# Token mixings: the first value weights lie where head outputs come later, and are queued ahead of the residual's stores and the stacking copies

## The chip, the core and the metric

The kernel runs on one core of a Trainium2 chip. The metric is the time of one execution in device microseconds (us), as the median of several runs. The engines are PE (matmul), DVE (vector), ACT (activation), POOL and SP; SP computes nothing here and issues the DMAs, one after the other.

## What is computed

The reference runs two residual blocks on 512 tokens of width 1024 and then two layers of a second network. Each of these layers is a feed-forward block, a token mixing and a second feed-forward block. The change touches the token mixing, which runs twice (mixing 0 and mixing 1):

```python
def token_mixing(h, w_in, rel_bias, lq1, lk1, lq2, lk2, subln_g, w_out, lambda_init):
    proj = h @ w_in
    qa, ka, va, qb, kb, vb, qc, kc, vc = jnp.split(proj, ...)
    o_a = chunk_band_attention(qa, ka, va, rel_bias)                       # 6 heads of 64
    o_b = diff_attention(qb, kb, vb, lam, subln_g, lambda_init)            # 4 heads of 64
    o_c = stick_breaking_attention(qc, kc, vc)                             # 6 heads of 64
    y = jnp.concatenate([o_a, o_b, o_c], axis=-1)
    return y @ w_out
```

The result is normed and added to the residual x, and the second feed-forward block follows.

## The kernel before

Activations lie with the features on the partitions: x is 8 tiles of 128 x 512 tokens. Every operand of a matmul is split into a high and a low part (xH and xL, wh and wl), and each product is three matmuls (`mm3`, L141 to L146: high by high, low by high, high by low).

**Weights.** All weights of the program stand in one list in the order of their use. `wload` (L74) loads the list up to a given entry, and `wnext` (L124) takes the next entry and loads four ahead. An entry is two tiles of 128 x 1024 (512 KB each), wh and wl, from a ring of five pairs; a load waits until the matmuls of the entry five before it have read their tiles. The weights of the mixings were split into halves earlier and stored in DRAM, so an entry of a mixing is two plain DMAs (L87), both issued by SP. In this text w0 to w3 are the first four entries of a mixing (the query and key weights of the head pairs 0 and 1), w4 to w7 the value weights of the first eight heads, and w8 the query weight of head pair 2.

**The start of a mixing** (`mix`, L1103). While the tail of the feed-forward block before it still updates x on DVE, PE does the projections with w0 to w3 (`head4`, L325, tile names p), in two halves of the tokens. SP stores the new x to DRAM (L1113, eight DMAs of 256 KB, spill), since the value tile V takes the memory of x. Each projection is then scaled on DVE (qkf, L1138), split by ACT and DVE (hl, L233 and L234) and copied, high and low parts stacked on 128 partitions, to the tiles sq and sk by SP's DMAs (`stack`, L1132): 24 copies of 128 KB for the first four projections. Only two hl tiles are there, so the third split waits for the copies of the first.

**The value projection** (`vproj`, L1161, tile names pv) uses w4 to w7 twice, for each half of the tokens: 2 x 48 matmuls of 512 columns into two PSUM banks, which ACT and DVE empty into V (L1177, L1178) after each half.

**The heads.** Each head has score matmuls (pS, L1186, 8 of them), maxima on DVE (L1209), exponentials on ACT (L1225), 10 transposes on PE (pT, L1245), a split of the transposed probabilities on ACT and DVE (pH, pL) and the output matmuls (pO, L1256). The projections of later heads (pq) are interleaved with the steps of the heads. The outputs of a head pair, split again, go to a tile O of 128 x 2 x 512. The first six, O0 to O5, are allocated at the start of the mixing:

```python
        O = {i: o_p.tile([P, 2, T], F32R, name=f"O{i}") for i in range(6)}
```

The order on each engine is set by a scheduler from the program and its dependencies, not by the order of the source alone.

Of the kernel before, what the change touches and what calls it, by code (L numbers as in the profile page):

```python
# [10 lines left out]
F32R = mybir.dt.float32r  # L11
# [6 lines left out]
P = 128  # L18
T = 512
# [8 lines left out]
def f(ap):  # L28
    return ap.bitcast(F32)


class Net:
# [6 lines left out]
    def __init__(s, ctx, tc, I, cols, dram):  # L39
        s.ctx, s.tc, s.nc, s.I, s.cols, s.dram = ctx, tc, tc.nc, I, cols, dram  # L40
        s.spill = dram.tile([P, 8, T], F32, name="spill")
        pool = lambda name, bufs=1, **k: ctx.enter_context(tc.tile_pool(name=name, bufs=bufs, **k))
        s.cp = pool("const")
        s.wp = pool("w", 5)
        s.xp = pool("x")
        s.ap = pool("acc")
        s.tp = pool("tiny", 2)
        s.pp = pool("ps", 1, space=PSUM)
        s.psum(mm=range(6), t=(6, 7))
        s.held, s.free = "x", "fb"  # L50
        s.wq, s.wi, s.ready, s.loaded, s.jobs, s.due, s.rate = [], 0, {}, 0, [], 0, 2.2
        s.early = []
        nc = s.nc
        s.w_eng = nc.vector
        s.ident = s.cp.tile([P, P], F32, name="ident")
        s.ones = s.cp.tile([P, P], F32, name="ones")
        nc.vector.memset(s.ones, 1.0)
        s.vecs = s.cp.tile([P, I["vecs"].shape[1]], F32, name="vecs")
        nc.sync.dma_start(s.vecs, I["vecs"])
# [14 lines left out]
    def wload(s, upto):  # L74
        nc = s.nc
        while s.loaded < min(upto, len(s.wq)):
            ap, n, hl = s.wq[s.loaded]
            if not hl:
                st = s.wp.tile([P, 1024], F32, tag="ws", name="ws", bufs=2)
                nc.sync.dma_start(st[:, :n], ap)  # L80
            wh = s.wp.tile([P, 1024], F32R, tag="wh", name="wh")
            wl = s.wp.tile([P, 1024], F32R, tag="wl", name="wl")
            s.ready[s.loaded] = (wh, wl)
            s.loaded += 1
            if hl:
                for x, w in enumerate((wh, wl)):
                    nc.sync.dma_start(f(w[:, :n]), hl[:, x])  # L87
                continue
            nc.scalar.activation(wh[:, :n], st[:, :n], AF.Copy)  # L89
            s.w_eng.tensor_tensor(wl[:, :n], st[:, :n], f(wh[:, :n]), op=ALU.subtract)  # L90
            s.due = s.due + s.rate if s.jobs else 0
            while s.jobs and s.due >= 1:
                s.jobs.pop(0)()
                s.due -= 1
# [706 lines left out]
    def cd(s, X, C):  # L801
# [122 lines left out]

        s.psum(S=range(3), T=(3, 4, 5), O=(6,), mm=(7,))
        ap = pool("cda")
# [70 lines left out]
        def pv(hf):  # L997
            h, half = hf // 2, hf % 2
            b = h % 2
            if half == 0:  # L1000
                pOs[h] = s.bank("pO", "O")
            pO = pOs[h]
# [100 lines left out]
    def mix(s, l, st, mktail):  # L1103
# [3 lines left out]
        op = ExitStack()  # L1107
        s.psum(mm=(0, 1), S=(2, 3, 4, 7), O=(5,), t=(6,))
        s.w_eng = nc.gpsimd
        o_p = op.enter_context(tc.tile_pool(name="mo", bufs=1, reuse_waits="tile"))  # L1110
        a_p = op.enter_context(tc.tile_pool(name="ma", bufs=1, reuse_waits="tile"))
        for k in range(8):
            nc.sync.dma_start(s.spill[:, k], s.x[:, k])  # L1113

# [5 lines left out]
        nlam = s.tp.tile([P, 1], F32, tag="nlam", name="nlam")  # L1120
        nc.vector.scalar_tensor_tensor(nlam, ll[:, 1:2], -lam0, ll[:, 0:1], op0=ALU.add, op1=ALU.subtract)

        O = {i: o_p.tile([P, 2, T], F32R, name=f"O{i}") for i in range(6)}
        V = {}
        qk = {}

        def hl():

            return a_p.tile([P, 2, T], F32R, tag="hl", name="hl", bufs=2)
# [99 lines left out]
        def pv_head(z, hd):  # L1229
            side = not 6 <= hd < 10  # L1230

            v = V[hd // 8][0]
            pO = s.bank("pO", "O")
            vt = lambda j: v[:, j, hd % 8].rearrange("p a d -> p (a d)")
# [26 lines left out]
        def o_add(pO, hd):  # L1261
            e, pr = hd % 2, hd // 2
            if e == 0:
                OT[pr] = a_p.tile([P, T], F32, tag="OT", name="OT", bufs=1)
            a, b = slice(64 * e, 64 * e + 64), slice(64 - 64 * e, 128 - 64 * e)
            o = OT[pr][a]
            nc.scalar.activation(o, pO[b], AF.Copy)
            nc.vector.tensor_tensor(o, pO[a], o, op=ALU.add)
            if e == 0:
                return  # L1270
            if pr < 5:
                bc = s.bcast2(rcs.pop(pr).rearrange("p i b -> p (i b)"), "t")
                nc.vector.tensor_tensor(OT[pr], OT[pr], bc, op=ALU.mult)
            if 3 <= pr < 5:
                sub_norm(pr)
            if pr >= 6:
                O[pr] = hl()
            s.split(O[pr][:, 0], O[pr][:, 1], OT[pr])

        def head_a(h):  # L1280
            tab = a_p.tile([P, T], F32, tag="tab", name="tab", bufs=2)
            nc.sync.dma_start(tab, s.I["rel"][l, h])
            z, nm = maxes(("a", h // 2), h % 2, 0, tab)
            yield
            rc(h)
            exps(z, nm, rcs[h // 2][:, :, h % 2])
            yield
            o_add(pv_head(z, h), h)

        def head_b(h):  # L1290
            tab = a_p.tile([P, T], F32, tag="tab", name="tab", bufs=2)
            nc.sync.dma_start(tab, s.I["alibi"][h])
            key = ("b", h // 2)
            m0 = maxes(key, h % 2, 0, tab)
            m1 = maxes(key, h % 2, 1, tab)
            yield
            z0, z1 = m0[0], m1[0]
            hd = 6 + h
            rc(hd)

            q = s.tp.tile([P, 4], F32, tag="rq", name="rq")
            s0 = exps(*m0, rcs[hd // 2][:, :, h % 2])
            exps(*m1, q)
            nc.vector.scalar_tensor_tensor(q, q, nlam, s0, op0=ALU.mult, op1=ALU.mult)
            for i in range(4):
                nc.vector.scalar_tensor_tensor(zs(z0, i), zs(z1, i), q[:, i:i + 1], zs(z0, i), op0=ALU.mult, op1=ALU.add)
            yield
            o_add(pv_head(z0, hd), hd)

        def sub_norm(pr):  # L1310
            ot = OT[pr]
            sq = s.ap.tile([P, T], F32, tag="md", name="osq")
            nc.scalar.activation(sq, ot, AF.Square)
            ps = s.bank("sn", "t")
            for t in range(4):
                nc.tensor.matmul(ps[:, 2 * t:2 * t + 2], sq[:, t * P:(t + 1) * P], s.hsel, start=True, stop=True)
            v = s.tp.tile([P, 8], F32, tag="snv", name="snv")
            nc.vector.tensor_scalar(v, ps[:, 0:8], 1.0 / 64, 1e-6, op0=ALU.mult, op1=ALU.add)
            y = s.rsqrt(v, 8, "sn")
            ps = s.bcast2(y, "t")  # L1320
            g = s.hg[f"subln_{l}"]
            nc.vector.scalar_tensor_tensor(ot, ot, g, ps, op0=ALU.mult, op1=ALU.mult)

        def head_c(h):
            key = ("c", h // 2)
            nb, be = ztile(), ztile()
            for i in range(4):
                n = (i + 1) * P
                ps = scores(key, h % 2, 0, i, stop=False)
                nc.tensor.matmul(ps[:, i * P:n], s.identr, s.maskr, start=False, stop=True)  # L1330
                nc.scalar.activation(zs(nb, i), ps[:, :n], AF.Sigmoid, scale=-1.0)
                nc.scalar.activation(zs(be, i), ps[:, :n], AF.Sigmoid)
                nc.gpsimd.memset(zs(nb, i, 1)[:, n:], 1.0)
            yield
            for i in range(4):
                nbi = zs(nb, i)
                nc.vector.tensor_tensor_scan(nbi[:, ::-1], nbi[:, ::-1], nbi[:, ::-1], 1.0, op0=ALU.mult, op1=ALU.bypass)
                nc.vector.tensor_tensor(zs(be, i), zs(be, i), zs(nb, i, 1)[:, 1:], op=ALU.mult)
            yield
            hd = 10 + h  # L1340
            o_add(pv_head(be, hd), hd)
# [288 lines left out]
```

## Time and profile before

| what | value |
|---|---|
| median of 3 runs | 2776.08 us (2770.22 to 2778.55) |
| profiled execution, its own time | 2773.9 us |
| its span in the profile | 2772.1 us |
| mean granted TensorE clock | 0.978 |
| PE busy | 2637.8 us, 95% |
| DVE, ACT, POOL busy | 1506.4, 1057.8, 322.3 us |
| chain that ended last | PE 76%, DVE 13%, ACT 3%, DMA 3% |

The span is the time from the first to the last instruction of the profiled execution; the difference of 1.8 us to its own time lies around it. The clock is a share of 2.4 GHz. A wait is the idle time of an engine just before an instruction, with what ended it in angle form ("<- DMA wh<-hl" is a load of a wh tile from hl in DRAM). "ws<-", "wh<-", "wl<-" name a DMA by the tile that it writes and what it reads.

### The profile page before, as it was taken

What the parts mean: (1) busy time and instruction counts of PE and PEld (TensorE: products, weight loads), DVE (VectorE), ACT (ScalarE), POOL (GpSimd) and SP (SyncE); (2) the same over time, 40 slices, a digit from 0 to 9 for tenths busy, and PEclk for the clock granted to TensorE, in tenths of its full rate; (3) what the DMA queues carried; (4) which work ended last, traced back from release to release, by engine and by line L of the source; (5) the groups of instructions that cost most, each with busy time, mean ns of one, the idle gap of its engine ahead of it and who ended that gap; (6) DMA issues with size and microseconds to landing.
All of it is one profiled execution on the core that took longest, in us unless ns stands there. A gap on an engine that the chain in (4) does not pass through costs nothing.

```text
span 2772.1 us, 36203 instructions
## 1 busy us (share of the span) xinstructions
PE 2637.8 (95%) x13676; PEld 2229.2 (80%) x13676; DVE 1506.4 (54%) x2886; ACT 1057.8 (38%) x1951; POOL 322.3 (12%) x300
## 2 busy tenths in 40 slices
PE   7898999998999998999999999999998998999998
PEld 6787987887888886877888888888886877888887
DVE  7885632888545353675853436634335467642334
ACT  4122543765443232444542224433223355432222
POOL 2324343002000020001200002000001000300000
PEclk9999999999999998999999999999999999999999
DMA  7353123005897246654693223962235665232321
GB/s 268 133 183 127 44 86 98 28 32 188 296 324 270 93 143 194 194 159 153 205 309 122 94 89 103 322 216 99 96 110 183 205 197 152 70 106 92 99 91 62
DMA packets 133966, 418.15 MB, mean 151 GB/s; under 512 B 17376, under 2 KB 20960, under 8 KB 133792
## 3 DMA queue, kind: packets, MB, share of 16 engines
q1 hardware_dynamic: 133792, 415.84, 45.3%
q8 instruction: 108, 1.77, 0.3%
q14 instruction: 66, 0.54, 0.1%
HBM read 314.32 MB, written 73.40 MB: 140 GB/s over the span
## 4 chain that ended last, share of the span: by engine, by line
PE 76%; DVE 13%; ACT 3%; issue 3%; DMA 3%; SPq 1%; POOL 0%; DVEq 0%; ACTq 0%; POOLq 0%
PE pd L146 6%; PE pd L145 6%; PE pd L144 6%; PE pg L144 5%; PE pg L145 5%; PE pg L146 5%; PE pu L145 5%; PE pu L146 5%; PE pu L144 5%; DVE junk L472 2%; PE pO L1256 1%; PE pq L144 1%; DVE x L310 1%; PE pq L145 1%; PE pq L146 1%
## 5 line engine op out<-in xcount | busy, mean ns | idle before, releaser
L89 ACT ACTIVATE wh<-ws 128x1024 fp32r<-128x1024 f32 (+2 forms) x335 | 345.6, 1034 | 865.5 <-PE pd L145 242.1
L90 DVE TENSOR_TENSOR wl<-ws,wh 128x1024 fp32r<-128x1024 f32 (+1 forms) x267 | 318.1, 1192 | 165.0 <-ACT wh L89 161.6
L144 PE MATMUL pg<-xH,wh 128*128 128x512 f32 x672 | 262.3, 390 | 0.0
L146 PE MATMUL pg<-xH,wl 128*128 128x512 f32 x672 | 261.7, 389 | 0.0
L145 PE MATMUL pg<-xL,wh 128*128 128x512 f32 x672 | 261.7, 389 | 0.0
L146 PE MATMUL pd<-hH,wl 128*128 128x512 f32 x632 | 249.7, 395 | 0.0
L144 PE MATMUL pd<-hH,wh 128*128 128x512 f32 x632 | 249.6, 395 | 0.0
L145 PE MATMUL pd<-hL,wh 128*128 128x512 f32 x632 | 249.6, 395 | 0.0
L145 PE MATMUL pu<-xL,wh 128*128 128x512 f32 x640 | 249.2, 389 | 0.0
L144 PE MATMUL pu<-xH,wh 128*128 128x512 f32 x640 | 249.1, 389 | 0.0
L146 PE MATMUL pu<-xH,wl 128*128 128x512 f32 x640 | 249.0, 389 | 0.0
L90 POOL TENSOR_TENSOR wl<-ws,wh 128x1024 fp32r<-128x1024 f32 (+1 forms) x68 | 171.1, 2522 | 328.7 <-ACT wh L89 320.9
L244 POOL TENSOR_TENSOR accf<-accf,sq 128x256 f32<-128x256 f32 x48 | 39.6, 846 | 1388.3 <-ACT sq L243 1388.3
L396 DVE TENSOR_TENSOR ht<-ht,pu 128x512 f32<-128x512 f32 x80 | 54.8, 685 | 183.4 <-PE pu L146 181.3
L146 PEld LDWEIGHTS pg<-xH,wl 128*128 128x128 f32 x672 | 126.1, 188 | 26.2
L144 PEld LDWEIGHTS pg<-xH,wh 128*128 128x128 f32 x672 | 126.2, 188 | 26.1
L145 PEld LDWEIGHTS pg<-xL,wh 128*128 128x128 f32 x672 | 126.2, 188 | 25.9
L146 PEld LDWEIGHTS pd<-hH,wl 128*128 128x128 f32 x632 | 118.6, 188 | 28.8
L145 PEld LDWEIGHTS pd<-hL,wh 128*128 128x128 f32 x632 | 118.6, 188 | 28.8
L144 PEld LDWEIGHTS pd<-hH,wh 128*128 128x128 f32 x632 | 118.6, 188 | 28.6
L144 PEld LDWEIGHTS pu<-xH,wh 128*128 128x128 f32 x640 | 120.1, 188 | 25.1
L146 PEld LDWEIGHTS pu<-xH,wl 128*128 128x128 f32 x640 | 120.1, 188 | 24.9
(616 smaller groups left out, 5978.5 us busy)
## 6 DMA issues: line engine op xcount, KB each, us to landing
ws<-ffn_gate SPq DMA_DIRECT2D x88, 512.0 KB, 3.5
ws<-ffn_up SPq DMA_DIRECT2D x88, 512.0 KB, 3.5
hl<-eh SPq DMA_DIRECT2D x64, 512.0 KB, 7.2
hl<-el SPq DMA_DIRECT2D x64, 512.0 KB, 6.8
ws<-ffn_down SPq DMA_DIRECT2D x64, 512.0 KB, 3.7
wh<-hl SPq DMA_DIRECT2D x64, 512.0 KB, 4.5
wl<-hl SPq DMA_DIRECT2D x64, 512.0 KB, 5.9
es<-wqk SPq DMA_DIRECT2D x32, 512.0 KB, 6.0
```

Of the source, the lines that this page charges most:

```text
L89: nc.scalar.activation(wh[:, :n], st[:, :n], AF.Copy)
L90: s.w_eng.tensor_tensor(wl[:, :n], st[:, :n], f(wh[:, :n]), op=ALU.subtract)
L144: mm(out, A[0], B[0], start=start, stop=False)
L145: mm(out, A[0], B[1], start=False, stop=False)
L146: mm(out, A[1], B[0], start=False, stop=stop)
L244: (eng or nc.gpsimd).tensor_tensor(acc[0], acc[0], sq, op=ALU.add)
L310: nc.vector.scalar_tensor_tensor(s.x[:, k, sl], fk, s.hg[post][:, k:k + 1], s.x[:, k, sl], op0=ALU.mult, op1=ALU.add)
L396: nc.vector.tensor_tensor(t, t, pu, op=ALU.mult)
L472: nc.vector.tensor_tensor_reduce(j, w, fbt[:, v * 1024:(v + 1) * 1024], 1.0, 0.0, op0=ALU.mult, op1=ALU.add, accum_out=dst[:, m, v:v + 1])
L1256: nc.tensor.matmul(o, vt(j), p[:, j, c0:], start=(x == 0 and j == 0), stop=(x == 1 and j == nj - 1))
```

## The change

At the start of a mixing the entries w4, w5 and w6 get homes of their own: the six tiles O0 to O5, two for each entry, under the name wV. The load of everything up to w7 is asked for there, ahead of the stores of x. The tiles of the outputs are allocated when a head pair is done, with the same tags, so in the memory that the weights leave. w7 takes the fifth pair of the ring.

```diff
--- before.py
+++ after.py
@@ -49,7 +49,7 @@
         s.psum(mm=range(6), t=(6, 7))
         s.held, s.free = "x", "fb"
         s.wq, s.wi, s.ready, s.loaded, s.jobs, s.due, s.rate = [], 0, {}, 0, [], 0, 2.2
-        s.early = []
+        s.early, s.homes = [], {}
         nc = s.nc
         s.w_eng = nc.vector
         s.ident = s.cp.tile([P, P], F32, name="ident")
@@ -78,8 +78,11 @@
             if not hl:
                 st = s.wp.tile([P, 1024], F32, tag="ws", name="ws", bufs=2)
                 nc.sync.dma_start(st[:, :n], ap)
-            wh = s.wp.tile([P, 1024], F32R, tag="wh", name="wh")
-            wl = s.wp.tile([P, 1024], F32R, tag="wl", name="wl")
+            if s.loaded in s.homes:
+                wh, wl = [b() for b in s.homes.pop(s.loaded)]
+            else:
+                wh = s.wp.tile([P, 1024], F32R, tag="wh", name="wh")
+                wl = s.wp.tile([P, 1024], F32R, tag="wl", name="wl")
             s.ready[s.loaded] = (wh, wl)
             s.loaded += 1
             if hl:
@@ -1109,6 +1112,10 @@
         s.w_eng = nc.gpsimd
         o_p = op.enter_context(tc.tile_pool(name="mo", bufs=1, reuse_waits="tile"))
         a_p = op.enter_context(tc.tile_pool(name="ma", bufs=1, reuse_waits="tile"))
+
+        for j in range(3):
+            s.homes[s.wi + 4 + j] = [(lambda i=i: o_p.tile([P, 1024], F32R, tag=f"O{i}", name="wV")) for i in (2 * j, 2 * j + 1)]
+        s.wload(s.wi + 8)
         for k in range(8):
             nc.sync.dma_start(s.spill[:, k], s.x[:, k])
 
@@ -1120,7 +1127,7 @@
         nlam = s.tp.tile([P, 1], F32, tag="nlam", name="nlam")
         nc.vector.scalar_tensor_tensor(nlam, ll[:, 1:2], -lam0, ll[:, 0:1], op0=ALU.add, op1=ALU.subtract)
 
-        O = {i: o_p.tile([P, 2, T], F32R, name=f"O{i}") for i in range(6)}
+        O = {}
         V = {}
         qk = {}
 
@@ -1273,8 +1280,7 @@
                 nc.vector.tensor_tensor(OT[pr], OT[pr], bc, op=ALU.mult)
             if 3 <= pr < 5:
                 sub_norm(pr)
-            if pr >= 6:
-                O[pr] = hl()
+            O[pr] = o_p.tile([P, 2, T], F32R, tag=f"O{pr}", name=f"O{pr}") if pr < 6 else hl()
             s.split(O[pr][:, 0], O[pr][:, 1], OT[pr])
 
         def head_a(h):
```

On SP, at the start of mixing 0 (hl_85 to hl_88 are the DRAM copies of w4 to w7, hl_89 of w8; spill is the store of x, tab a table of biases, sq and sk the stacking copies), the rows before are:

```order
L87 DMA wh<-hl_85 128x1024
L87 DMA wl<-hl_85 128x1024
L1282 DMA tab<-rel 128x512 x2
L1113 DMA spill<-x 128x512 x8
L87 DMA wh<-hl_86 128x1024
L87 DMA wl<-hl_86 128x1024
L1132 DMA sq<-hl 64x512 x4
L1132 DMA sk<-hl 64x512 x8
L1132 DMA sq<-hl 64x512 x4
L1132 DMA sk<-hl 64x512 x8
L87 DMA wh<-hl_87 128x1024
L87 DMA wl<-hl_87 128x1024
```

Behind these come the loads of w7 and w8. With the change the same place of SP's queue reads:

```order
L90 DMA wV<-hl_85 128x1024 x2
L90 DMA wV<-hl_86 128x1024 x2
L90 DMA wV<-hl_87 128x1024 x2
L90 DMA wh<-hl_88 128x1024
L90 DMA wl<-hl_88 128x1024
L1120 DMA spill<-x 128x512 x8
L1288 DMA tab<-rel 128x512 x2
L90 DMA wh<-hl_89 128x1024
L90 DMA wl<-hl_89 128x1024
L1139 DMA sq<-hl 64x512 x4
L1139 DMA sk<-hl 64x512 x8
```

w5, w6 and w7 moved ahead of the stores, the two tables behind them, and w8 to the place before the copies that w5 had. Behind these rows come the other 12 copies and the loads of the next four entries.

On PE, where the scores meet the value projection in mixing 0, the end of the scores before is this; ahead of it stand only 24 of the 96 value matmuls, 20 of the 24 scores of the heads 0 to 2 and the 10 transposes of head 0:

```order
L1186 MATMUL pS<-sk,sq 128x128
L1186 MATMUL pS<-sk,sq 128x256
L1186 MATMUL pS<-sk,sq 128x384
L1186 MATMUL pS<-sk,sq 128x512
L144 MATMUL pv<-wh,xH 128x512 x2
L145 MATMUL pv<-wl,xH 128x512
L146 MATMUL pv<-wh,xL 128x512
```

The other 72 value matmuls follow. With the change 48 value matmuls stand ahead of the first scores, here with the last three of them:

```order
L147 MATMUL pv<-wh,xH 128x512
L148 MATMUL pv<-wl,xH 128x512
L149 MATMUL pv<-wh,xL 128x512
L1193 MATMUL pS<-sk,sq 128x128 x2
L1193 MATMUL pS<-sk,sq 128x256 x2
L1193 MATMUL pS<-sk,sq 128x384 x2
L147 MATMUL pv<-wV,xH 128x512
L148 MATMUL pv<-wV,xH 128x512
L149 MATMUL pv<-wV,xL 128x512
```

Only 6 scores of head 0 lie between the two halves of the value projection; the other scores and the transposes of the first three heads moved behind it, between the matmuls of the next two projections (pq). Mixing 1 changes in the same way, and a few projections later the order is as before.

## Rows read from the trace of the kernel before

**Rows 1.** Busy time by stretch: us, PE, PEld, DVE, ACT, POOL, PEclk, DMA share, GB/s.
```profile
1055.50:1101.00 45.50, 35.94 (x131) 26.41 (x132) 13.98 (x43) 12.71 (x35) 0.00 (x0) 0.81 0.75 216
2111.40:2156.00 44.60, 35.12 (x133) 25.55 (x134) 14.07 (x43) 12.72 (x36) 0.00 (x0) 0.85 0.74 218
...
1101.00:1201.00 100.00, 99.27 (x546) 83.42 (x545) 58.91 (x162) 41.74 (x110) 0.00 (x0) 1.00 0.60 187
```

**Rows 2.** Waits of PE, 1055 to 1102: us in total, times, longest.
```profile
PE pv L144 <- DMA wh<-hl: 3.4, 2, 3.1
PE pv L145 <- DMA wl<-hl: 2.8, 2, 2.1
PE pT L1245 <- ACT z L1225: 1.2, 1, 1.2
```

**Rows 3.** Timeline of SP's queue, loads of mixing 0: start, us, instruction.
```profile
1020.22 0.32 SPq L87 DMA_DIRECT2D wh<-hl  x1
...
1022.36 0.32 SPq L87 DMA_DIRECT2D wh<-hl  x1
...
1053.64 0.32 SPq L87 DMA_DIRECT2D wh<-hl  x1
...
1075.19 0.53 SPq L87 DMA_DIRECT2D wh<-hl  x1
...
1079.02 0.83 SPq L87 DMA_DIRECT2D wl<-hl  x1
```

**Rows 4.** Timeline of PE, ends of the stretch: start, us, instruction [idle before].
```profile
1055.48 0.50 PE L144 MATMUL pv<-wh,xH 128*128 128x512 f32 x1
...
1089.90 0.50 PE L144 MATMUL pv<-wh,xH 128*128 128x512 f32 x1 [0.89 <-DVE V L1178]
...
1100.91 0.28 PE L1256 MATMUL pO<-pH,V 128*128 128x256 f32 x1
...
2111.38 0.50 PE L144 MATMUL pv<-wh,xH 128*128 128x512 f32 x1
...
2155.76 0.34 PE L1256 MATMUL pO<-pH,V 128*128 128x256 f32 x2
```

**Rows 5.** Timeline of PE, 7 transposes and 8 scores with what follows each.
```profile
1109.98 0.38 PE L1245 MATMUL pT<-ident,z 128*128 128x128 f32 x2
...
1110.66 0.47 PE L144 MATMUL pq<-xH,wh 128*128 128x512 f32 x1
...
1122.41 0.39 PE L1186 MATMUL pS<-sk,sq 128*128 128x128 f32 x2
...
1123.74 0.39 PE L144 MATMUL pq<-xH,wh 128*128 128x512 f32 x1
```

**Rows 6.** Timeline of PE, first and last scores ahead of w6.
```profile
1065.66 0.39 PE L1186 MATMUL pS<-sk,sq 128*128 128x128 f32 x2
...
1075.72 0.95 PE L1186 MATMUL pS<-sk,sq 128*128 128x384 f32 x2
```

**Rows 7.** Timelines of PE and DVE: w3's first matmul, the wait for the sums.
```profile
1024.85 0.28 PE L144 MATMUL p<-xH,wh 128*128 128x256 f32 x1
...
1026.56 0.16 DVE L290 SCALAR_TENSOR_TENSOR vffn_post<-tsffn_post,wcdr 128x2 f32<-128x2 f32 x1 [0.99 <-PE tsffn_post L207]
```

**Rows 8.** DMA issues at 1020.22, 1075.19, 1079.02 in turn: KB, us to landing.
```profile
wh<-hl SPq DMA_DIRECT2D x1, 512.0 KB, 4.2
...
wh<-hl SPq DMA_DIRECT2D x1, 512.0 KB, 4.5
...
wl<-hl SPq DMA_DIRECT2D x1, 512.0 KB, 8.7
```

**Rows 9.** Busy time by stretch, as in rows 1.
```profile
1075.00:1085.00 10.00, 6.18 (x15) 4.08 (x15) 0.18 (x1) 0.71 (x3) 0.00 (x0) 0.50 0.92 277
...
1201.00:1300.00 99.00, 87.26 (x476) 71.96 (x475) 73.25 (x169) 54.88 (x141) 3.32 (x27) 0.97 0.58 173
```

**Rows 10.** Chain that ended last, a value matmul right after a wait: start, us.
```profile
1082.50 0.43 PE pv L146
```

## The prediction

> **What bounds the kernel now.** I read the page first, then the waits of PE in the two token mixings, then their rows in order of time, then the DMA queue of SP. PE, the matmul engine, carries the chain that ended last, so a change is worth what it takes out of PE's idle or slow time on that chain. Much of a mixing leaves nothing to take: from 1101 to 1201 in mixing 0 PE is busy 99.27 of 100 us [rows 1]. The stretch from the first value matmul to the first output matmul is the exception. It lasts 45.5 us in mixing 0 and 44.6 us in mixing 1, and the granted clock averages 0.81 and 0.85 there, between its two levels of 1.2 and 2.4 GHz [rows 1]. The largest waits inside it are for weights: in mixing 0 3.4 us for wh halves and 2.8 us for wl halves [rows 2]. The reader should see in SP's queue why: the second value weight w5 is issued at 1053.64, and w6 only at 1075.19 [rows 3], when PE had begun the value projection at 1055.48 [rows 4]. Between the two stand the 24 stacking copies, which wait for ACT and DVE.
>
> The named waits are 6.2 us in mixing 0, but that is not the price of the stretch. While PE waits for w6 it does the scores and transposes of heads 0 to 2, each step of which waits for DVE or ACT, and after the waits it runs at the low clock. So I price the whole stretch against the same work done without gaps.
>
> **The change, part by part.**
>
> *The stretch.* Mixing 0: from 1055.48 to 1100.91 are 45.43 us; mixing 1: from 2111.38 to 2155.76 are 44.38 us [rows 4]. The work in either is 96 value matmuls, 24 score matmuls (8 for each of three heads) and 10 transposes. Their undisturbed price in this trace:
> - value matmuls: 48 of them from 1089.90 to 1100.91 [rows 4], 11.01 us or 0.2294 each; 96 take 22.02 us;
> - scores: 8 from 1122.41 to 1123.74, 1.33 us [rows 5]; 24 take 3.99 us;
> - transposes: 7 from 1109.98 to 1110.66 [rows 5], 0.097 each; 10 take 0.97 us.
>
> Together 26.98 us. What is over is 45.43 - 26.98 = 18.45 us in mixing 0 and 17.40 us in mixing 1, 35.85 us in all. With all four value weights loaded long before 1055.48 and the scores queued behind the value matmuls, neither the wait for a weight nor the empty time between the steps of a head has a place on PE; nor has the low clock that came with them.
>
> *What is late next.* Three waits may take the place of the removed one. First, 6 score matmuls stand in the middle of the value projection. PE reaches them at 1055.48 + 48 x 0.2294 = 1066.49; in the trace the same scores ran at 1065.66 without a wait [rows 6], so their copies had landed, with at least 0.8 us to spare. They also cover part of the time in which ACT and DVE empty the first two banks, for which PE stood 0.89 us before [rows 4]. Second, the transposes of head 0 wait for exponentials, 1.2 us in the trace [rows 2]; now projection matmuls stand between them. Third, the output matmuls of head 0 now come soon after its exponentials and may wait for ACT and DVE to split its probabilities; before, some 25 us lay between, so no row here has this wait. From below, none of this costs anything, since projection matmuls are spread between the steps, as in the 100 us in which PE lost 0.73 us in all [rows 1]. From above, the whole chain of three heads is bare again as it was: it took from 1065.66 to 1075.72 + 0.95 = 1076.67 [rows 6], 11.01 us for 4.96 us of work, so 6.05 us. I take 0.89 + 1.2 = 2.1 us per mixing, because the new neighbourhood is nearer to the dense 100 us than to the bare chain. That is 4.2 us for both.
>
> *The queue of SP.* Six loads of 512 KB (w5 to w7) move ahead of the eight residual stores; w6 and w7 thereby pass the 24 copies too, and w8 takes the place that w5 had just before them. The new wait is that memory which the feed-forward block held must have been read for the last time; w4's load had such a wait and was issued at 1022.36 [rows 3], and I take the same for the new ones. Behind them on SP stand the stores, and these wait for DVE's last update of the residual in any case, so a few us of issue ahead of them cost nothing; the cover is that update. The data costs DMA time: in a burst of six such loads the first, issued at 1075.19, landed after 4.5 us and the last, issued at 1079.02, after 8.7 us [rows 3, 8], so 8.0 us for five more, 1.6 us each. All eight value loads (w4 to w7) take 12.8 us behind w3, which landed at 1020.22 + 4.2 = 1024.42 [rows 3, 8]: they are in by 1037.2, and PE wants the first at 1055.48. If that cover were gone, the late loads would cost what they do now. The stores come behind them, but the tile they free is first written after half of the value projection, at 1066.49. The two tables move behind the stores and are read after the scores, at the same time. Before the copies one pair is loaded as before (now w8, then w5), so the copies should land as they did.
>
> *The projection ahead.* PE uses w3 first at 1024.85 [rows 7], 0.43 us after it lands. Behind that matmul on PE stand the sums for which DVE's residual tail waits: it stood idle 0.99 us for them until 1026.56 [rows 7]. If the new loads made w3 late, all of the tail would move with it. In the burst the loads landed in the order of issue, so I take nothing. The upper bound is that w3 lands with the last of the new loads, at 1037.2: 12.4 us per mixing. The Trainium skill, page "DMA: Bandwidth & Descriptors", section "Two DMAs through the same engine are not ordered", says that nothing orders DMAs across the 16 engines, which allows this; by it at its worst the sum is 2767.1 us, and the landings in order of issue in rows 8 speak against it.
>
> *Other edits.* The first outputs are allocated later, in the tiles that the weights leave. Their first write comes after the value projection, so its cover is whole and it costs nothing. No instruction is added on PE, ACT, DVE or POOL.
>
> *The sum.* 35.85 - 4.2 = 31.6 us off the profiled execution's 2773.9 us: **2742.3 us**. The median of the three runs, 2776.08, is 2.2 us above that execution, and the runs reach from 2770.22 to 2778.55; I keep 4 us on either side for that.
>
> **The rivals.**
> - *The heads lose their cover.* DVE and ACT cannot keep up with the heads once PE does not wait for weights, and the 6.05 us of the bare chain return in place of 2.1. For it: the scores, exponentials and splits of three heads now fall into the time of two projections. Against it: the dense 100 us, in which the same steps ran between projections. 2773.9 - 35.85 + 12.1 = **2750.2 us**.
> - *Given back later.* From 1201 to 1300 PE is busy only 87.26 of 99 us [rows 9]. If the pace there is DVE's and does not move with the earlier start, up to 11.7 us per mixing go: 2742.3 + 23.4 = **2765.7 us**. Against it: the work of DVE there hangs on projections that PE would finish earlier.
> - *w3 is late*, by the 12.4 us above: 2742.3 + 24.8 = **2767.1 us**. The order of landings speaks against it.
> - *Slower: the clock.* PE waits in the residual tail just ahead of the value projection. If the clock fell there and stayed down through the stretch, a value matmul would take 0.43 us [rows 10] instead of 0.2294, and the 26.98 us of work 26.98 x 0.43 / 0.2294 = 50.6 us, 23.6 us more per mixing: 2742.3 + 47.2 = **2789.5 us**. The point from which the kernel is slower than before is two thirds of the stretch at the low level (31.6 of 47.2 us). For it: the clock granted from 1075 to 1085 was 0.50 [rows 9], its low level. Against it: that stretch came right after a wait, and the 48 value matmuls from 1089.90 on were fast again [rows 4] once PE had worked without a gap.
>
> **How the numbers follow.** The forecast has 0.74, the heads' chain 0.12, given back later 0.06, w3 late 0.04, the clock 0.04. About 0.3% (8.3 us) is what a measurement of this kernel can tell from no change. The forecast and the heads' chain are faster by more than that: 0.86. Given back later and w3 late end just within it: 0.10. The clock ends slower by more than that: 0.04. The range begins at the sum without any new wait, 2738.1, less 4 us: 2734. It ends at the bare chain, 2750.2, plus 4 us and rounded up: 2755. What lies outside is the last three cases and a little of the first two, not over 2 in 10.
>
> **What would show each step.** Right: the eight value loads issued within about 4 us of w3, ahead of the stores; no wait of the value matmuls for a DMA; the 96 value matmuls plus 6 scores done some 23 to 24 us after their start, at a granted clock near 1.00; the later half of each mixing unchanged but 15 to 16 us earlier relative to the projection. Wrong: PE waiting for w3 near the start of the first projection (then w3 is late); waits of transposes or output matmuls above 2 us in all during the next two projections (then the chain); value matmuls of 0.43 us (then the clock); or more than 11.7 us of PE idle in the later half (then given back).

## The result, and the profile after

| what | before | after |
|---|---|---|
| median (runs) | 2773.82 us (4) | 2743.84 us (4) |
| lowest to highest | 2770.22 to 2778.55 us | 2740.75 to 2744.86 us |
| span of the profiled execution | 2772.1 us | 2741.7 us |
| mean granted clock | 0.978 | 0.980 |

The ratio of after to before is 0.9889, with a 95% interval from 0.987 to 0.9908: faster by 30.0 us in the medians and by 30.4 us in the profiled spans. Lines of the changed kernel are numbered 3 to 7 higher (mm3 L147 to L149, scores L1193, transposes L1252, output matmuls L1263).

The loads first. SP's queue in mixing 0, in order of time (start, us, instruction), the counterpart of [rows 3]:

```profile
1018.34 0.32 SPq L90 DMA_DIRECT2D wh<-hl  x1
1018.75 0.38 SPq L90 DMA_DIRECT2D wl<-hl  x1
1019.18 4.57 SPq L90 DMA_DIRECT2D wV<-hl  x6
1023.80 0.65 SPq L90 DMA_DIRECT2D wh<-hl  x1
1025.33 0.32 SPq L90 DMA_DIRECT2D wl<-hl  x1
1032.15 0.32 SPq L1120 DMA_DIRECT2D spill<-x  x1
```

The sizes of the first two loads (w3) and of the last one (w7) in KB, and their us from issue to landing, the counterpart of [rows 8]:

```profile
wh<-hl SPq DMA_DIRECT2D x1, 512.0 KB, 3.8
...
wl<-hl SPq DMA_DIRECT2D x1, 512.0 KB, 6.6
...
wl<-hl SPq DMA_DIRECT2D x1, 512.0 KB, 11.8
```

w3 is whole at 1018.75 + 6.6 = 1025.4, and the last value weight at 1025.33 + 11.8 = 1037.1, 15 us before PE wants the first one. PE's timeline shows that no value matmul waits; these are the ends of the two halves of the value projection in mixing 0 and of the whole in mixing 1, the counterpart of [rows 4, 6]:

```profile
1052.22 0.50 PE L147 MATMUL pv<-wV,xH 128*128 128x512 f32 x1
...
1063.44 0.97 PE L1193 MATMUL pS<-sk,sq 128*128 128x128 f32 x6
...
1075.76 1.43 PE L1193 MATMUL pS<-sk,sq 128*128 128x512 f32 x8
...
2093.45 0.50 PE L147 MATMUL pv<-wV,xH 128*128 128x512 f32 x1
...
2116.95 0.96 PE L1193 MATMUL pS<-sk,sq 128*128 128x512 f32 x5
```

96 value matmuls and 6 scores take 1075.76 - 1052.22 = 23.54 us, and 23.50 us in mixing 1. In all of PE's waits from 1052 to 1098 only one is left; it takes the place of [rows 2], and mixing 1 has the same one:

```profile
PE pO L1263 <- ACT pH L236: 0.2, 1, 0.2
```

To compare equal work, the stretch must end where both kernels have done the same. That is the first matmul of the third later projection (pq): up to there the records of mixing 0 hold 96 value matmuls, 24 scores, 23 transposes, 24 output matmuls and 48 projection matmuls in either kernel. I call it the **equal stretch**. By stretch, the kernel before (columns as in [rows 1]; the first and the fourth row are the projection with w0 to w3, the second and the fifth the equal stretch, the third and the sixth the part from the tenth later projection to the output projection, the last the output projection to the sums of the norm):

```profile
1023.09:1055.48 32.39, 28.80 (x224) 28.05 (x223) 25.47 (x73) 13.03 (x33) 10.30 (x13) 0.95 0.39 139
1055.48:1117.44 61.96, 52.20 (x223) 40.30 (x224) 21.73 (x57) 17.51 (x44) 0.00 (x0) 0.86 0.73 222
...
1207.49:1263.11 55.62, 47.65 (x267) 39.11 (x265) 46.42 (x109) 32.63 (x83) 0.99 (x20) 0.94 0.55 162
...
2080.37:2111.38 31.01, 27.29 (x224) 26.53 (x224) 25.47 (x73) 13.03 (x33) 10.30 (x13) 1.00 0.42 147
2111.38:2172.30 60.92, 51.26 (x224) 39.30 (x224) 21.82 (x57) 17.38 (x44) 0.00 (x0) 0.89 0.73 225
...
2262.36:2317.84 55.48, 47.48 (x266) 39.13 (x265) 46.38 (x109) 32.63 (x83) 1.06 (x20) 0.94 0.53 155
2317.84:2370.02 52.18, 48.20 (x283) 41.26 (x282) 23.66 (x45) 23.62 (x56) 10.64 (x14) 1.00 0.49 162
```

The changed kernel, the same seven:

```profile
1021.21:1052.22 31.01, 27.28 (x224) 26.53 (x223) 25.46 (x73) 13.03 (x33) 10.29 (x13) 1.00 0.68 249
1052.22:1097.30 45.08, 44.77 (x225) 36.48 (x224) 21.32 (x56) 17.17 (x44) 0.00 (x0) 1.00 0.78 234
...
1187.37:1243.79 56.42, 48.95 (x267) 40.37 (x265) 46.41 (x109) 32.63 (x83) 1.00 (x20) 0.91 0.55 161
...
2060.72:2093.45 32.73, 28.96 (x225) 28.04 (x224) 25.48 (x73) 13.04 (x33) 10.30 (x13) 0.95 0.65 236
2093.45:2138.54 45.09, 44.78 (x223) 36.46 (x224) 21.35 (x56) 17.16 (x44) 0.00 (x0) 1.00 0.78 233
...
2228.61:2284.94 56.33, 48.83 (x266) 40.26 (x265) 46.23 (x109) 32.63 (x83) 1.07 (x20) 0.91 0.53 153
2284.94:2339.59 54.65, 49.86 (x283) 42.55 (x281) 23.94 (x45) 23.70 (x56) 10.64 (x14) 0.97 0.47 154
```

The reader should see three things. The equal stretch fell from 61.96 to 45.08 us and from 60.92 to 45.09 us, 32.71 us in all, and the clock in it rose from 0.86 and 0.89 to 1.00. In mixing 0 PE's idle time there went from 9.76 to 0.31 us, so 9.45 of the 16.88 us are waits; the other 7.43 us are busy time for the same matmuls. Most of that is the clock. In the kernel before, it was at its low level in these two parts of the stretch:

```profile
1062.13:1065.54 3.41, 3.41 (x10) 2.63 (x9) 1.31 (x2) 0.63 (x1) 0.00 (x0) 0.50 0.83 207
1072.37:1086.02 13.65, 9.34 (x24) 6.44 (x25) 1.69 (x5) 2.94 (x10) 0.00 (x0) 0.50 0.92 268
```

PE was busy 12.75 us in them, half of which, 6.4 us, the full clock would have saved. And the other stages moved by little, in both directions:

| stage | gain in mixing 0 | in mixing 1 |
|---|---|---|
| projection with w0 to w3 | 1.38 | -1.72 |
| equal stretch | 16.88 | 15.83 |
| third to tenth later projection | -0.02 | -0.01 |
| tenth later projection to output projection | -0.80 | -0.85 |
| output projection to the norm's sums | -0.12 | -2.47 |

Ahead of mixing 0 the changed kernel was already 1.88 us earlier, and between the mixings it gained 0.45 us. The sum of it all is 30.4 us.

### The profile page after: what moved, and what is told of

It reads as the page before. It is cut to its first block, busy times and chain, and to the rows that moved or that the text cites. A ratio compares the mean times of both kernels' runs of the same rounds, so it can differ in the third digit from the quotient of the medians.

```text
span 2741.7 us, 36211 instructions
## 1 busy us (share of the span) xinstructions
PE 2632.7 (96%) x13676; PEld 2230.8 (81%) x13676; DVE 1504.3 (55%) x2886; ACT 1056.6 (39%) x1951; POOL 323.0 (12%) x300
## 5 line engine op out<-in xcount | busy, mean ns | idle before, releaser
L147 PE MATMUL pg<-xH,wh 128*128 128x512 f32 x672 | 262.2, 390 | 0.0
L149 PE MATMUL pg<-xH,wl 128*128 128x512 f32 x672 | 261.7, 389 | 0.0
L149 PE MATMUL pd<-hH,wl 128*128 128x512 f32 x632 | 249.6, 395 | 0.0
L147 PE MATMUL pd<-hH,wh 128*128 128x512 f32 x632 | 249.6, 395 | 0.0
L147 PE MATMUL pu<-xH,wh 128*128 128x512 f32 x640 | 249.1, 389 | 0.0
L149 PE MATMUL pu<-xH,wl 128*128 128x512 f32 x640 | 249.0, 389 | 0.0
L149 PEld LDWEIGHTS pg<-xH,wl 128*128 128x128 f32 x672 | 126.1, 188 | 26.1
L147 PEld LDWEIGHTS pg<-xH,wh 128*128 128x128 f32 x672 | 126.2, 188 | 26.1
L149 PEld LDWEIGHTS pd<-hH,wl 128*128 128x128 f32 x632 | 118.6, 188 | 28.8
L147 PEld LDWEIGHTS pd<-hH,wh 128*128 128x128 f32 x632 | 118.6, 188 | 28.7
L147 PEld LDWEIGHTS pu<-xH,wh 128*128 128x128 f32 x640 | 120.1, 188 | 25.0
L148 PEld LDWEIGHTS pu<-xL,wh 128*128 128x128 f32 x640 | 120.1, 188 | 24.9
```

Of the source, the lines that this page charges most:

```text
L147: mm(out, A[0], B[0], start=start, stop=False)
L148: mm(out, A[0], B[1], start=False, stop=False)
L149: mm(out, A[1], B[0], start=False, stop=stop)
```

## The experiments

All times are medians, with the ratio to the kernel before on the same chip; its medians there were 2776.59, 2775.11 and 2777.05 us. In each, "equal stretch" is as above.

**1. Early weights, old order on PE.** The changed kernel, in which PE must do what it did before; for that the first head's transposes are cut off from its output matmuls.

```diff
-        for g in range(2):
-            for _ in vproj(0, g):
...
+        v0 = vproj(0, 0)
+        for _ in range(8):
+            next(v0)
+        for h in (0, 0, 1, 0, 2):
+            next(heads[h])
+        with tc.issue_after(last[0]):
+            for _ in v0:
                 pass
+            for _ in vproj(0, 1):
+                pass
```

> The value weights stay as early as in the changed kernel, but PE is made to do what it did before: 24 value matmuls, then all 24 scores of heads 0 to 2 and the 10 transposes of head 0, then the other 72 value matmuls. Theory of the forecast (the wait for weights and the bare steps of the heads both cost time): the stretch is 24 x 0.2294 = 5.5 us, 11.0 us of the bare chain, 16.5 us for 72 value matmuls and 1 to 4 us until the stacking copies of head 0 are there, 34 to 37 us against 23.7 us of the same work in the changed kernel plus some 3.3 us of its scores and transposes: 7 to 10 us more per mixing, 2758 to 2764 us. If only the arrival of the weights counts, it stays at 2744 us. If only the order on PE counts, it is back at 2774 us.

Measured: 2761.89 us, 0.9952 (0.9937 to 0.9967). By stretch, the equal one of each mixing and the scores alone:

```profile
1054.89:1110.02 55.13, 51.18 (x224) 40.65 (x224) 22.07 (x57) 17.15 (x44) 0.00 (x0) 0.88 0.65 193
2104.61:2159.38 54.77, 49.71 (x223) 39.79 (x224) 22.07 (x57) 17.26 (x44) 0.00 (x0) 0.91 0.66 192
...
1061.00:1075.00 14.00, 10.50 (x35) 7.59 (x36) 7.99 (x27) 7.12 (x22) 0.00 (x0) 0.65 0.75 173
```

PE's timeline has four waits at the bare heads; the first is for a stacking copy, and none is for a weight:

```profile
1062.90 0.64 PE L1193 MATMUL pS<-sk,sq 128*128 128x128 f32 x3 [2.15 <-DMA sk<-hl]
1064.09 4.35 PE L1193 MATMUL pS<-sk,sq 128*128 128x512 f32 x13 [0.55 <-DVE qkf L1145]
1069.51 1.99 PE L1250 MATMUL pT<-ident,z 128*128 128x128 f32 x7 [0.43 <-ACT z L1232]
1072.91 1.97 PE L1193 MATMUL pS<-sk,sq 128*128 128x512 f32 x5 [0.58 <-DVE pL L237]
```

With every weight there, the old order still costs 10.05 and 9.68 us per mixing. The waits are only 3.7 us of that in mixing 0; PE is busy 6.4 us longer than in the changed kernel (51.18 against 44.77), with a clock of 0.65 around the scores (from 1065.29 to 1078.94 it is at its low level, 0.50, and PE is busy 12.60 us, half of which is 6.3 us). So less than half of the gain is the arrival of the weights by itself.

**2. Late weights, new order on PE.** w6 and w7 go behind the copies, and all scores behind the value projection (in the changed kernel 6 of them stand in its middle).

```diff
-        s.wload(s.wi + 8)
+        s.wload(s.wi + 6)
...
+        with tc.issue_after(copies[-1]):
+            s.wload(s.wi + 4)
...
-        next(heads[0])
-        next(heads[0])
+        with tc.issue_after(s.last):
+            next(heads[0])
+            next(heads[0])
```

> The loads of w6 and w7 are put behind the 24 stacking copies again (issued near 1071 us), while the scores are held behind the whole value projection, as the changed kernel has them nearly. Theory of the forecast: PE waits from its 24th value matmul (some 1058 us) to the landing of w6 (some 1076 us) with nothing to do, 18 us per mixing, and goes on at the low clock: 2744 + 36 to 48 = 2780 to 2792 us, slower than before the change, because before PE did scores in that wait. If the order on PE alone makes the gain, it stays near 2744 us.

Measured: 2779.42 us, 1.0018 (1.0009 to 1.0027), just below the range that the theory gave and the only one above the kernel before. The profiled execution took 2786.15 us. The equal stretch of mixing 0 (that of mixing 1 takes 63.10 us), and PE's waits in it:

```profile
1059.03:1122.29 63.26, 47.38 (x224) 37.95 (x224) 21.53 (x57) 17.37 (x44) 0.00 (x0) 0.87 0.66 204
...
PE pv L147 <- DMA wV<-hl: 14.5, 1, 14.5
PE pv L147 <- DVE V L1187: 0.9, 1, 0.9
PE pv L148 <- DMA wV<-hl: 0.3, 1, 0.3
```

The wait for the weights stands bare: 14.5 us, against 6.2 us in the kernel before, which had the scores to do meanwhile. The new order pays nothing by itself.

**3. Late weights, order left to the scheduler.** As in experiment 2, without the last part of its diff.

> As the run before with w6 and w7 behind the copies, but nothing is said about the order on PE, so the scheduler sets it; it puts the scores of heads 0 to 2 behind 24 value matmuls, as before the change. The tiles O0 to O5 are still the homes of w4 to w6, and w4 and w5 are still loaded early. Theory of the forecast (place in the queue, not memory, is what pays): all of the gain is gone, 2770 to 2777 us. If the homes or the later allocation of the outputs had a value of their own, it would be below 2768 us.

Measured: 2773.74 us, 0.9989 (0.9976 to 1.0002). On PE 24 value matmuls, the 24 scores with the 10 transposes, and 72 value matmuls follow each other as before the change. The equal stretch of mixing 0 (that of mixing 1 takes 57.94 us):

```profile
1054.82:1113.85 59.03, 50.55 (x224) 38.93 (x224) 21.56 (x57) 17.50 (x44) 0.00 (x0) 0.88 0.71 219
```

In this execution the stretches are 2.9 and 3.0 us shorter than before the change; in the medians the homes alone, with w5 early and w6 and w7 late, are worth no more than can be measured. With the same late weights the new order of experiment 2 takes 4.2 and 5.2 us more in the two stretches.

**4. Mixing 0 alone.**

```diff
-        for j in range(3):
+        for j in range(3 * (l == 0)):
...
-        s.wload(s.wi + 8)
+        if l == 0:
+            s.wload(s.wi + 8)
```

> The change is made in mixing 0 alone. Theory of the forecast: the mixings do not touch each other, mixing 0 gives its 15 to 18 us and mixing 1 keeps its old stretch of 44 to 45 us: 2756 to 2759 us, and from the first value matmul to the third of the later projections mixing 0 takes 45 us as in the changed kernel, mixing 1 61 us as before. If the gain came partly from elsewhere (the 1.9 us by which the changed kernel was ahead already at the first mixing, or a saving in the feed-forward blocks), the time differs from the half by over 3 us.

Measured: 2759.26 us, 0.9951 (0.9934 to 0.9968). The equal stretches, changed in mixing 0 and as before in mixing 1:

```profile
1053.30:1098.33 45.03, 44.73 (x223) 36.45 (x224) 21.32 (x56) 17.16 (x44) 0.00 (x0) 1.00 0.78 235
2091.50:2152.12 60.62, 51.36 (x223) 39.13 (x224) 21.75 (x57) 17.51 (x44) 0.00 (x0) 0.89 0.73 226
```

The gains add up: each mixing gives its own.

**5. The changed kernel again.** No edit.

> The changed kernel itself once more, on the chip of the next three runs, for a second profile. From the first value matmul to the third later projection 45.1 us in both mixings again; what lies behind that stretch (some 0.8 us before the output projection in either mixing and 2.5 us behind its start in mixing 1, lost against the kernel before) comes back if the change caused it, and is elsewhere or gone if it was chance. 2741 to 2747 us.

Measured: 2741.41 us, 0.9884 (0.9868 to 0.9899). The equal stretches take 45.03 and 45.07 us. The 2.47 us behind the start of the output projection in mixing 1 were chance; that part now takes less than before the change:

```profile
2284.41:2335.75 51.34, 48.25 (x282) 41.23 (x281) 23.92 (x45) 23.62 (x56) 10.64 (x14) 1.00 0.51 164
```

The part before the output projection takes 56.48 us in both mixings, 0.86 and 1.00 us more than before the change, so by itself this run would put the loss down to the change. Experiment 4 speaks against it. There the same part of the changed mixing 0 is shorter than in the kernel before (55.62 us), and that of the unchanged mixing 1 is longer (before, 55.48 us):

```profile
1188.36:1243.47 55.11, 47.38 (x267) 38.77 (x265) 46.42 (x109) 32.62 (x83) 0.99 (x20) 0.94 0.57 167
2242.53:2300.03 57.50, 50.22 (x267) 41.75 (x265) 46.37 (x109) 32.62 (x83) 1.06 (x20) 0.88 0.52 151
```

So this part varies from execution to execution by more than it moved, and it is longer where its granted clock is lower: 0.94 in 55.11 us, 0.91 in 56.42, 0.88 in 57.50.

**6. Two homes.**

```diff
-        for j in range(3):
+        for j in range(2):
...
-        s.wload(s.wi + 8)
+        s.wload(s.wi + 7)
```

> Only w4 and w5 get homes; w6 takes the fifth pair of the ring and w7 the pair that w0 leaves, so w7 is issued behind the stores and the two tables, but ahead of the stacking copies. Theory (only the place ahead of the copies counts): w7 lands some 10 us before PE wants it, and the time is that of the changed kernel within 3 us, 2741 to 2747 us. If the place ahead of the stores counts, PE waits for w7 in the value projection and several us per mixing are lost, 2750 us or more.

Measured: 2748.58 us, 0.9903 (0.989 to 0.9917): 7.2 us over the changed kernel, outside what was expected. No wait for a weight appears from 1054 to 1248. Among PE's waits there are some that the changed kernel of experiment 5 has not:

```profile
PE pS L1193 <- DVE mx L1216: 1.2, 2, 0.8
PE pv L147 <- DVE V L1185: 0.9, 1, 0.9
```

From the first value matmul to the output projection it takes 193.46 us in mixing 0, against 191.54 us, and 2.7 us more in mixing 1. The scheduler ordered the later heads otherwise, and DVE is waited for. Some waits of the changed kernel are shorter here, so that PE's idle time in mixing 0 is 9.64 us against 8.54; the other 0.8 us of the 1.92 is busy time. The two mixings make 4.6 us; the rest lies in stages that vary from run to run, and is not settled.

**7. One home.**

```diff
-        for j in range(3):
+        for j in range(1):
...
-        s.wload(s.wi + 8)
+        s.wload(s.wi + 6)
```

> Only w4 gets a home; w5 takes the fifth pair, w6 the pair of w0 and is issued ahead of the copies, w7 behind them. The scheduler now puts the scores of heads 0 to 2 behind 36 value matmuls. Theory: PE loses the bare steps of the heads (10 us per mixing as with early weights and the old order) and 1 to 3 us for w7: 55 to 58 us from the first value matmul to the third later projection, 2762 to 2768 us. If the gain grew with each weight that is early, two thirds of the way from the kernel before to the changed one would be two weights and this one half: 2758 us.

Measured: 2770.85 us, 0.9985 (0.9975 to 0.9994), outside what was expected, and slower than both theories. PE's waits for weights in mixing 0 (the 0.3 us of the second row that are not in its longest wait are for w6, ahead of the scores):

```profile
PE pv L147 <- DMA wh<-hl: 3.3, 1, 3.3
...
PE pv L148 <- DMA wl<-hl: 1.7, 2, 1.4
```

The scores stand behind 36 value matmuls. The bare heads and a wait of 4.7 us for the last weight together leave 60.11 and 57.85 us of the equal stretch. The gain is not in proportion to the weights that are early: w5 and w6 bring 4.3 us here, and w7 the other 29. Only in the runs in which w7 too is ahead of the copies, and whose order was left to the scheduler, does it put 48 value matmuls ahead of the first scores and all but 6 scores behind the value projection.

**8. Value matmuls in the gap**, a step further. PE waits 2.7 us for the norm's factors in the projection with w0 to w3, before and after the change. With the value weights early, value matmuls can stand behind it. The factors are spread over the partitions later: in mixing 0 those of the first half come behind 48 matmuls of the projection, and those of the second behind 24 of them and 6 value matmuls.

```diff
         y = s.rsqrt(v, 2, nm)
+        yield
         b = s.bcast(y, 2, nm)
...
-            pv = [s.bank("pv") for _ in range(2)]
+            pv = [s.bank("pv", "mm" if h or g else "S") for _ in range(2)]
...
-        p0 = s.head4(st, ("mm", "mm", "S", "S"), (10, 13))
+        p0 = s.head4(st, ("mm", "mm", "S", "S"), (10, 13, 14, 16))
+        v0 = vproj(0, 0)
+        for _ in range(2):
+            next(v0)
+        st["w"].append(next(st[1]))
```

The steps of `at` (10, 13, 14, 16) are those of the sums and of the spreading of either half, which a second `yield` parts.

> A further step: with the value weights there early, the first value matmuls are put into the time in which PE waits 2.7 us for the norm's factors at the end of the projection with w0 to w3. The factors are spread over the partitions later on PE (behind 48 and 30 matmuls instead of 20 and 14), and the first half of the value projection uses two PSUM banks of the scores' group, so that it needs not wait for the projection's results to be scaled. Theory: the 2.7 us go in both mixings, and with them the 1.4 us of low clock that follow them in some executions: 5.5 to 8 us less than the changed kernel, 2735 to 2739 us. Rival: the stacking copies then start as late as now while the scores come earlier on PE, so the wait only moves and the time is that of the changed kernel.

Measured: 2730.05 us, 0.9834 (0.9821 to 0.9848), against 0.9884 for the changed kernel in experiment 5: 11.4 us less, the fastest of all. Projection and equal stretch of both mixings (4 of the matmuls that spread the factors are now in the latter):

```profile
1025.25:1052.38 27.13, 26.25 (x221) 26.05 (x220) 24.79 (x72) 12.63 (x31) 10.30 (x13) 1.00 0.76 275
1052.38:1097.31 44.93, 44.70 (x229) 36.89 (x228) 22.10 (x57) 17.80 (x45) 0.00 (x0) 1.00 0.80 240
2062.74:2089.84 27.10, 26.50 (x220) 26.09 (x220) 24.72 (x72) 12.63 (x31) 10.35 (x13) 1.00 0.77 276
2089.84:2134.85 45.01, 44.80 (x229) 36.88 (x228) 22.13 (x57) 17.79 (x45) 0.00 (x0) 1.00 0.81 239
```

The projections took 31.03 and 32.73 us in experiment 5 and take 27.13 and 27.10 us here, 9.5 us less, and the equal stretch gives none of it back: the two stages together are 4.0 us shorter in mixing 0 and 5.7 us in mixing 1. The wait for the factors did not move. PE's idle time fell by 2.9 and 3.0 us. The rest is busy time: 2.7 us in mixing 1, where the clock of the projection rose from 0.95 to 1.00, and 1.1 us in mixing 0, where it was 1.00 in both runs. The theory's 5.5 to 8 us had the wait and the low clock in them; why PE is also 1.1 us less busy at the same clock is not settled.

The profiled execution took 2737.87 us, 7.8 us over the median and only 2.1 us below the profiled one of experiment 5: it begins mixing 0 at 1025.25 and not at 1020.74, and from the norm's sums of mixing 0 to mixing 1 it takes 767.80 us and not 765.06. Experiment 2's, without this edit, has 1026.47 and 768.08 us there, so neither is put down to the edit. That value matmuls must be early for this gain is not shown: only 6 of them stand ahead of a spreading, the first half's wait is covered by the projection's own matmuls, and the later spreading alone was not run.

Instead PE now waits 0.9 us for w3:

```profile
PE p L149 <- DMA wl<-hl: 0.9, 1, 0.9
```

**9. Homes without the request.** `s.wload(s.wi + 8)` is taken out of the changed kernel, nothing else.

> The three homes stay, but nothing asks for the loads at the start of the mixing; they are asked for where they were before the change, in the source behind the stores and for w5 to w8 behind the copies. With memory of its own the scheduler still puts w4, w5 and half of w6 ahead of the stores, the other half of w6 in the middle of them and w7 behind them, all ahead of the stacking copies. Theory (what counts is the place ahead of the copies): PE waits for no weight in the value projection, and the time is that of the changed kernel, 2740 to 2747 us; as with two homes, a few us more are possible from the later order of the heads alone. If the place ahead of the stores is worth something by itself, PE shows waits for wV or wh in the value projection and loses over 3 us per mixing, 2750 us or more.

Measured: 2742.41 us, 0.9875 (0.9858 to 0.9891), the time of the changed kernel. The equal stretch of mixing 0 (that of mixing 1 takes 45.12 us):

```profile
1054.52:1099.56 45.04, 44.73 (x223) 36.47 (x224) 21.31 (x56) 17.16 (x44) 0.00 (x0) 1.00 0.78 234
```

Here w7 and half of w6 come amid or behind the stores. For these loads the place ahead of the stores is worth nothing, and so is the explicit request. With the three homes the scheduler by itself puts all value weights ahead of the copies; that place makes the change, as experiment 3, with the same homes and w6 and w7 behind the copies, shows from the other side.

## Why the prediction was right

Forecast were 2742.3 us within 2734 to 2755; measured were 2743.84 and, on another chip, 2741.41 us. That the first is within 1.5 us is in part luck: the stretch gave 1.1 us more than forecast, and the stages that the forecast left out lost 2.3 us in that execution. By its steps:

- **The stretch** (35.85 us over dense work, less new waits of 4.2, so 31.6 us). The equal stretch gave 32.71 us. Dense, it would be the 26.98 us of the forecast and what stood behind that in the kernel before, 1117.44 - 1100.91 = 16.53 us, 43.51 us; it took 45.08. The 1.57 us over it stand against the 2.1 us of new waits, but they are something else. PE is idle 0.31 us in either stretch, and neither transposes nor output matmuls wait over 0.2 us; so the waits nearly vanished, and the dense price was 1.3 us too low. Of that the 96 value matmuls are 0.47 us: 11.22 and 11.27 us for the two halves, not 11.01 each. The two errors, 1.8 and 1.3 us per mixing, mostly cancel; that too is luck.
- **The price against dense work, not the named waits.** This step carried the forecast. By the named waits for weights, 6.2 us in mixing 0 [rows 2] and taken as much for mixing 1, it would have been some 12 us. The view of the waits does name most of the idle time, 9.6 us in mixing 0 if those of the heads, of DVE and of ACT are added, but not the low clock. Four runs with w5 early show why the step was right: equal stretches in mixing 0 of 59.03 us (w6 and w7 late, old order, experiment 3), 55.13 (early, old, experiment 1), 63.26 (late, new, experiment 2) and 45.08 (early, new). Early weights bring 3.9 us in the old order and 18.2 us in the new one. What the forecast did not say is that the new order without the weights costs 4.2 us, and that all weights early in the old order bring 6.8 of the 16.88 us.
- **The heads' chain** as a rival did not come about, but its price was too low: 6.05 us, against 10 us in experiment 1. There the chain itself, from 1062.90 to 1074.67, is 6.8 us over its dense price; 2.15 us more are the wait for a stacking copy, and some 2.0 us the low clock that it brings to the ten value matmuls behind it (4.27 us for 2.29).
- **Given back later** was taken as nothing, with 11.7 us per mixing as its worst. The part ahead of the output projection lost 0.80 and 0.85 us here, but it took 55.11 us in a changed mixing and 57.50 us in an unchanged one in experiment 4. No loss by the change is shown, and at the most it is about 1 us per mixing.
- **The queue of SP.** The last value load was in at 1037.1, where 1037.2 was worked out; the agreement is luck. The high half of w3 landed at 1022.1 and not at 1024.42, and the eight loads took 15.0 us behind it, not 12.8. They were issued in 7.0 us from w3's first load on, and not in 4. That w7 and half of w6 are ahead of the stores is irrelevant (experiment 9).
- **w3** was taken as not late, from its wh half alone. Its wl half, just ahead of the new loads, needed 6.6 us to land; before the change it needed 5.2, as this row of the kernel before shows (its issue at 1020.64):

```profile
wl<-hl SPq DMA_DIRECT2D x1, 512.0 KB, 5.2
```

  No matmul waited for it in either profile of the changed kernel. In experiment 8 it needed 7.9 us and one waited 0.9 us, and in four other runs (experiments 1, 2, 6 and 9) one waited 0.3 to 0.5 us; the rival has a small part of its price in these, not 12.4 us. The Trainium skill, page "DMA: Bandwidth & Descriptors", section "Two DMAs through the same engine are not ordered", gives no order across the 16 engines; here w3 and w7, first and last, landed in the order in which they were issued.
- **The clock** did not stay low: 1.00 in both equal stretches, although PE waits 2.7 us shortly before. That rival's price was never tested; experiment 1 shows 0.65 around the bare scores.

The 1.88 us ahead of mixing 0 and the differences in the projection with w0 to w3 belong to no step. Over all profiled runs mixing 0 begins between 1020.5 and 1026.5. The projection took 31.0 us at a clock of 1.00 or 32.4 to 32.7 us at 0.95, in both kernels once each.

## What to carry to other kernels

Price a stretch with waits at what the same instructions take undisturbed elsewhere in the trace, and not at the sum of its named waits: waits gave back 9.45 us and busy time, most of it low clock, 7.43 us here where the view of the waits named 6.2 us for weights. Where a scheduler sets the order, ask which of its inputs flips it: of the three weights that were late, two early ones gave 4.3 us, and the last one the other 29. And then look for the next wait that matmuls at hand can cover; spreading the norm's factors later brought another 11 us here.

## What was not expected of the hardware

The same 2.7 us wait of PE for the norm's factors is followed by a granted clock that differs from mixing to mixing of one execution. From that wait to the first value matmul the changed kernel took 6.73 us in mixing 0 (1045.49 to 1052.22), and in mixing 1 this row, with a clock of 0.81:

```profile
2085.28:2093.45 8.17, 8.01 (x53) 7.64 (x53) 2.41 (x13) 0.79 (x3) 0.00 (x0) 0.81 0.12 38
```

In the kernel before it was the other way round, 8.09 us in mixing 0 (1047.39 to 1055.48) and 6.73 us in mixing 1 (2104.65 to 2111.38). Why the clock falls in one and not in the other is not settled; experiment 8, in which PE does not wait there, has 1.00 in both.
